# Query and gate strips of 512 columns, and one right operand for the high and low halves

## The chip, the cores and the metric

The kernel runs on one core of a Trainium2 chip. The metric is the device time of one execution in microseconds, the median of several runs. The profile is of one more execution, taken by the hardware profiler. Its engines are TensorE (PE, with its weight loads shown as PEld), VectorE (DVE), ScalarE (ACT), GpSimd (POOL) and SyncE (SP, which here issues the DMAs).

## What is computed

One encoder layer is applied to two sequences: a prompt of 1024 tokens and a sample of 256 tokens, both with the same 16 meta tokens in front. The outputs for the meta tokens are dropped.

```
u = rms_norm(h, norm_w) @ w_in                      # (tokens, 2048) @ (2048, 6656)
qa, ka, va, za, qb, kb, vb, zb = split(u)           # 8, 2, 2, 8, 8, 8, 8, 8 heads of 128
qa, ka = rope(rms_norm(qa)), rope(rms_norm(ka))
ya = softmax(qa ka^T) va * silu(za)                 # global, 4 query heads share a key head
qb, kb = rms_norm(qb), rms_norm(kb)
yb = neighbourhood(qb, kb, vb, bias) * silu(zb)     # window of 8 x 16 tokens, and the meta tokens
y = h + concat(ya, yb) @ w_out
```

Keys and values of the meta tokens are needed. Their queries and gates (z) are not, because their outputs are dropped.

## The kernel before

The input projection is made of 52 strips. A strip is one head's 128 columns of `w_in`, loaded as 16 weight tiles of 128 x 128 (`KT` = 16, the contraction over 2048). The tokens stand in the columns of the right operand. The projection goes over the tokens twice. Chunk one (`chunk1`, line 616) holds 512 columns: the sample's 256 tokens, the prompt's first 240, and the 16 meta tokens at the end. Chunk two (`chunk2`, line 759) holds the prompt's other 784 tokens (`T2`), in a block of 512 and one of 272 (`BL`, line 769), because a PSUM tile of the projection holds 512 columns.

To keep accuracy, each float32 operand is split into a high part in float32r and a low part, the remainder, also in float32r (`split`, line 64). A product is three matmuls into the same PSUM tile: high weights by high x (line 227), high weights by low x (line 228) and low weights by high x (line 229). `strips` (line 192) holds these lines: for each of four weight groups `c` of `WCH` = 4 tiles, for each block `b`, for each of the four tiles `k`, three matmuls.

In chunk one the x tiles are made by `get_x` (line 104) as one tile of `[P, 2, T1]`, high in the first half and low in the second, aligned to 128 bytes. All strips read the first columns of it: k and v strips take all 512 (`B0`, line 636), q and z strips the first 496 (`BQ`). In chunk two `load_all_x` (line 153) makes two tiles for each of the 16 k: `ta` with high and low of the 512 block, and `tb` of 560 columns (`NX`) with the high part of the 272 block in front and the low part in its last 272 columns, from column 288.

A strip's evacuation follows its matmuls. q and k strips go through `qk_evac` (line 257: square, sum over partitions on GpSimd, rotation, reciprocal square root, split), z strips through `z_evac` (line 299: the gate by Exp and Ln), v strips through `v_rows` and transposes. Their results are kept in SBUF or stored to DRAM for later. The PSUM pool `pp` of the projection has four tiles, so a strip of chunk two, which takes two, has its evacuation under the next strip's matmuls.

The order of the work: `chunk1` projects strips and puts the sample's attention of a head between later strips (`later`, `put`, `run_due`). `chunk2` projects, head by head, z and q of the eight global heads, each followed by the head's attention (`attend`, line 366) and one strip of the local heads as filler (`fill`); then come the remaining local strips with the local heads' attention placed between them (`attend_strip`, line 463). The output projection follows (`outproj`, line 1107). The framework's scheduler orders each engine's instructions from this program order, with explicit constraints (`issue_after`, `place_after`). SP issues all the loads and stores in one queue.

The functions that the change touches and what calls them:

Of the kernel before, what the change touches and what calls it, by code (L numbers as in the profile page):

```python
# [21 lines left out]
P = 128  # L22
# [8 lines left out]
T1 = NMETA + NS + C1P  # L31
T2 = NP - C1P
NB = 512
# [26 lines left out]
class Kern:  # L60
# [92 lines left out]
    def load_all_x(self):  # L153
# [3 lines left out]
        for kt in range(KT):  # L157
# [5 lines left out]
            for h, l in ((ta[:, 0], ta[:, 1]), (tb[:, :NT2], tb[:, NX - NT2:])):  # L163
# [9 lines left out]
                o += n  # L173
        self.tc.add_manual_dep(self.qstore, self.xload[KT // 2].name, mybir.DependencyInfo(
# [17 lines left out]
    def strips(self, jobs, getx):  # L192
# [4 lines left out]
        for c in range(KT // WCH):  # L197
# [22 lines left out]
            for b in range(nb)[::-1] if self.turn else range(nb):  # L220
                for k in range(WCH):
                    kt = c * WCH + k
                    xh, xl = getx(kt)[b]
                    first, last = kt == 0, kt == KT - 1
                    for (wh, wl), ps, (_, blocks, _) in zip(ws, out, jobs):
                        p, n = ps[b], blocks[b][1]
                        nc.tensor.matmul(p[:, :n], wh[:, k, :], xh[:, :n], start=first, stop=False)  # L227
                        nc.tensor.matmul(p[:, :n], wh[:, k, :], xl[:, :n], start=False, stop=False)  # L228
                        self.lastmm = nc.tensor.matmul(p[:, :n], wl[:, k, :], xh[:, :n], start=False, stop=last).ins  # L229
# [300 lines left out]
    def rows_out(self, vt, n, dst, o):  # L530

        nc = self.nc
        for a in range(0, n, 4 * P):
# [10 lines left out]
            if f < len(offs):  # L544
# [3 lines left out]
                nc.sync.dma_start(dst[o + n - m:o + n], t[:])  # L548
# [67 lines left out]
    def chunk1(self):  # L616
# [19 lines left out]
        B0, BQ = (0, T1), (0, NS + C1P)  # L636
        PM = NS + C1P

        def kb_strip(s, g, wc):
            kf = self.k.tile([P, T1], F32, tag="k1", name="kcf")  # L640

            def evac(ps):
                self.qk_evac(ps[0], 0, T1, wc, None, [], kf[:])
                nc.sync.dma_start(self.kfd[g][:], kf[:, NS:])
                km = self.k.tile([P, 8, NMETA], F32, tag="km", name="kmf")[:, :3]
                nc.scalar.copy(km, kf[:, PM:].unsqueeze(1).to_broadcast([P, 3, NMETA]))
                return kf, km.rearrange("p c m -> p (c m)")
# [13 lines left out]
        def k_strip(s, g, wc, rope):  # L661
            kt_ = self.k.tile([P, 2, T1], F32R, tag="k1", name="kc1")

            def evac(ps):
                self.qk_evac(ps[0], 0, T1, wc, (ct, st) if rope else None, [(0, T1, kt_[:, 0, :], kt_[:, 1, :])])
                nc.sync.dma_start(self.kd[g][:], kt_[:, :, NS:].bitcast(F32))
                return kt_, self.copy_km(kt_[:, :, PM:])
            return s, [B0], evac

        def v_strip(s, g):  # L670
# [4 lines left out]
            def evac(ps):  # L675
                vt = self.v_rows(ps[0], *B0)
                self.split(vm[:, 0:1, :], vm[:, 1:2, :], self.v_turn(vt, [PM], NMETA))
                if loc:
                    nc.scalar.copy(vs[:], self.v_turn(vt, [0, P]))
                else:  # L680
                    self.split(vs[:, :2, :], vs[:, 2:, :], self.v_turn(vt, [0, P]))
                self.rows_out(vt[:, NS:PM], C1P, self.vn[g], 0)
# [5 lines left out]
        def q_strip(s, h, wc, rope):  # L688
            q = self.s.tile([P, 2, QB], F32R, tag="S", name="qs")

            def evac(ps):
                o, n = BQ
                qp = [self.ev.tile([P, C1P], F32R, tag="ev", name="qp") for _ in range(2)]
                self.qk_evac(ps[0], o, n, wc, (ct[:, o:o + n], st[:, o:o + n]) if rope else None,
                             [(0, NS, q[:, 0, :], q[:, 1, :]), (NS, C1P, qp[0][:], qp[1][:])])
# [5 lines left out]
        def z_strip(s, h):  # L701
            z = self.zlater = self.mx.tile([P, QB], F32, tag="mx", name="zs")

            def evac(ps):
                zp = self.ev.tile([P, C1P], F32, tag="ev", name="zp")
                self.z_evac(ps[0], *BQ, [(0, NS, z[:]), (NS, C1P, zp[:])])
                nc.sync.dma_start(self.zd[h][:, :C1P], zp[:])
# [51 lines left out]
    def chunk2(self):  # L759
# [9 lines left out]
        BL = [(0, NB), (NB, T2 - NB)]  # L769
        self.tie = 0, 0  # L770

# [8 lines left out]
        def k_strip(s, g, wc, rope):  # L780
            k, km = k_first(g)

            def evac(ps):
                for p, (o, n) in zip(ps, BL):
                    rp = (ct[:, o:o + n], st[:, o:o + n]) if rope else None
                    self.qk_evac(p, o, n, wc, rp, [(0, n, k[:, 0, C1P + o:C1P + o + n], k[:, 1, C1P + o:C1P + o + n])])
# [3 lines left out]
        def v_rows_of(s, g):  # L790

            def evac(ps):
                for p, (o, n) in zip(ps, BL):
                    self.rows_out(self.v_rows(p, o, n), n, self.vn[g], C1P + o)
# [21 lines left out]
        def q_strip(s, h, wc, rope):  # L816
            q = self.q.tile([P, 2, NP], F32R, tag="q", name="q", align_bytes=ALIGN)
            nc.sync.dma_start(q[:, :, :C1P].bitcast(F32), self.qd[h][:])

            def evac(ps):  # L820
                for p, (o, n) in zip(ps, BL):
                    rp = (ct[:, o:o + n], st[:, o:o + n]) if rope else None
                    self.qk_evac(p, o, n, wc, rp, [(0, n, q[:, 0, C1P + o:C1P + o + n], q[:, 1, C1P + o:C1P + o + n])])
                return q
            return s, BL, evac

        def z_strip(s, h):
            z = self.z.tile([P, NP], F32, tag="z", name="z")
            nc.sync.dma_start(z[:, :C1P], self.zd[h][:, :C1P])

            def evac(ps):
                for p, (o, n) in zip(ps, BL):
                    self.z_evac(p, o, n, [(0, n, z[:, C1P + o:C1P + o + n])])
                return z
            return s, BL, evac


        def qk_late(s, wc, dst):
            def evac(ps):
                for p, (o, n) in zip(ps, BL):  # L840
                    self.qk_evac(p, o, n, wc, None, [(0, n, dst[:, o:o + n], None)])
            return s, BL, evac

        def z_late(s, dst):
            def evac(ps):
                for p, (o, n) in list(zip(ps, BL))[::-1 if self.turn else 1]:
                    zt = self.ev.tile([P, n], F32, tag="ev", name="zt")
                    self.z_evac(p, o, n, [(0, n, zt[:])])
                    nc.sync.dma_start(dst[:, C1P + o:C1P + o + n], zt[:])
            return s, BL, evac  # L850
# [12 lines left out]
        def q_load(h):  # L863
            qf = self.qf.tile([P, NP], F32, tag="qf", name="qfull")
            nc.sync.dma_start(qf[:, :C1P], self.qfd[h][:])
            nc.sync.dma_start(qf[:, C1P:], self.q2d[h][:])
# [65 lines left out]
        for h in range(NH):  # L932
            v = [v_rows_of(VB + h, 2 + h)]
            kq = [qk_late(KB + h, kwb, self.k2d[2 + h]), qk_late(QB_ + h, qwb, self.q2d[8 + h])]
# [252 lines left out]
    def build(self):  # L1187
# [3 lines left out]
        with tc.tile_pool(name="dr", bufs=1, space=DRAM) as dp, tc.tile_pool(name="const", bufs=1) as cp, \  # L1191
# [5 lines left out]
            self.qd = [dp.tile([P, 2, C1P], F32, name=f"qd{h}") for h in range(8)]  # L1197
            self.qfd = [dp.tile([P, C1P], F32, name=f"qfd{h}") for h in range(16)]
# [145 lines left out]
```

## Time and profile before

| what | value |
|---|---|
| median of 3 runs | 2160.34 us (2159.44 to 2160.65) |
| the profiled execution, its time | 2159.27 us |
| its span in the profile | 2157.5 us |
| granted clock of TensorE | 1.00 |
| PE busy in the span | 2151.3 us |
| DVE, ACT, POOL busy | 1658.5, 1189.0, 522.3 us |

The profile's rows name a line of the kernel, an engine, an operation and its tiles as out<-in, then the shape (partitions x elements), how many there are, the busy time and the mean nanoseconds of one. Matmuls are pipelined: one starts well before the one ahead of it has ended, so the duration of one (390 ns for 512 columns) is no measure of the rate. The distance from one start to the next is. A timeline gives the starts, and its first column is the start in us from the beginning of the span.

### The profile page before, as it was taken

To read this page: it belongs to the slowest core of one execution; us is meant where nothing else is said; L and a number is where in the kernel's file an instruction comes from. 1 tells how busy PE (TensorE), PEld (TensorE's weight loads), DVE (VectorE), ACT (ScalarE), POOL (GpSimd) and SP (SyncE) were. 2 spreads that over 40 slices of the span, in tenths; PEclk is the share of its full clock that TensorE was granted. 3 is DMA by queue.
4 is the path that set the end of the run, shared out by engine and by line. 5 is a ranking of instruction groups with operands and counts; after the bars stand their busy time and mean duration, and the time that the engine had idled before them with its cause. 6 is when DMAs were issued, how large, how long until landed. Compare 5 with 4: busy or idle time off the path is not lost.

```text
span 2157.5 us, 33972 instructions
## 1 busy us (share of the span) xinstructions
PE 2151.3 (100%) x11745; PEld 1877.5 (87%) x11745; DVE 1658.5 (77%) x2989; ACT 1189.0 (55%) x2411; POOL 522.3 (24%) x250
## 2 busy tenths in 40 slices
PE   9999999999999999999999999999999999999999
PEld 7888888888888999999999999998989988888887
DVE  7698976788874899997799998677787886545763
ACT  7677644454565777776677775444443464232230
POOL 1142422222221223231143224324333311000000
PEclk9999999999999999999999999999999999999999
DMA  8666789988664333334332344654443364662663
GB/s 294 216 192 221 241 297 313 331 288 265 214 193 137 94 105 104 106 105 135 98 107 93 104 127 146 188 158 136 130 132 123 115 212 142 239 235 92 234 224 108
DMA packets 257420, 377.24 MB, mean 175 GB/s; under 512 B 43072, under 2 KB 108768, under 8 KB 257248
## 3 DMA queue, kind: packets, MB, share of 16 engines
q1 hardware_dynamic: 257248, 375.07, 53.6%
q8 instruction: 92, 1.51, 0.3%
q14 instruction: 80, 0.66, 0.1%
HBM read 281.01 MB, written 100.38 MB: 177 GB/s over the span
## 4 chain that ended last, share of the span: by engine, by line
PE 99%; DMA 0%; DVE 0%; SPq 0%; issue 0%; ACT 0%
PE pp L227 22%; PE pp L229 22%; PE pp L228 22%; PE pq L1069 6%; PE pq L1068 6%; PE pq L1070 6%; PE po L519 2%; PE sp L485 2%; PE sp L378 1%; PE sp L379 1%; PE sp L377 1%; PE po L420 1%; PE po L419 1%; PE po L418 1%; PE tp L540 0%; PE sp L430 0%
## 5 line engine op out<-in xcount | busy, mean ns | idle before, releaser
L227 PE MATMUL pp<-x,wh 128*128 128x512 f32 (+1 forms) x1664 | 655.0, 395 | 0.9 <-ACT wh L66 0.9
L229 PE MATMUL pp<-x,wl 128*128 128x512 f32 (+1 forms) x1664 | 647.6, 390 | 0.0
L228 PE MATMUL pp<-x,wh 128*128 128x512 f32 (+1 forms) x1664 | 647.1, 389 | 0.0
L229 PEld LDWEIGHTS pp<-x,wl 128*128 128x128 f32 x1664 | 312.4, 188 | 60.9 <-DVE wl L67 0.2
L227 PEld LDWEIGHTS pp<-x,wh 128*128 128x128 f32 x1664 | 312.3, 188 | 59.0 <-ACT wh L66 3.1
L228 PEld LDWEIGHTS pp<-x,wh 128*128 128x128 f32 x1664 | 312.8, 188 | 52.1
L67 DVE TENSOR_TENSOR wl<-wr,wh 128x512 fp32r<-128x512 f32 (+2 forms) x287 | 215.5, 753 | 122.2 <-ACT wh L66 91.3
L262 POOL PARTITION_ALL_REDUCE m<-ms x78 | 222.4, 2852 | 354.3 <-ACT ms L260 293.1
L346 POOL PARTITION_ALL_REDUCE tot<-a x80 | 179.2, 2240 | 435.4 <-DVE a L343 417.1
L66 ACT CAST wh<-wr 128x512 fp32r<-128x512 f32 (+2 forms) x287 | 173.7, 610 | 184.2 <-PE pp L228 170.4
L228 PE MATMUL pp<-xb,wh 128*128 128x272 f32 x832 | 240.7, 289 | 0.0
L227 PE MATMUL pp<-xb,wh 128*128 128x272 f32 x832 | 239.8, 288 | 0.0
L229 PE MATMUL pp<-xb,wl 128*128 128x272 f32 x832 | 239.1, 287 | 0.0
L328 POOL PARTITION_ALL_REDUCE ma<-m x80 | 114.4, 1429 | 448.4 <-DVE m L326 439.7
L1068 PE MATMUL pq<-wm,yh 128*128 128x512 f32 x560 | 218.3, 390 | 0.0
L1070 PE MATMUL pq<-wm,yl 128*128 128x512 f32 x560 | 218.2, 390 | 0.0
L1069 PE MATMUL pq<-wm,yh 128*128 128x512 f32 x560 | 218.0, 389 | 0.0
L227 PEld LDWEIGHTS pp<-xb,wh 128*128 128x128 f32 x832 | 156.5, 188 | 7.5
L228 PEld LDWEIGHTS pp<-xb,wh 128*128 128x128 f32 x832 | 156.5, 188 | 7.5
L229 PEld LDWEIGHTS pp<-xb,wl 128*128 128x128 f32 x832 | 157.4, 189 | 0.3
L1068 PEld LDWEIGHTS pq<-wm,yh 128*128 128x128 f32 x560 | 105.1, 188 | 21.8
L1070 PEld LDWEIGHTS pq<-wm,yl 128*128 128x128 f32 x560 | 105.1, 188 | 21.8
(214 smaller groups left out, 3932.1 us busy)
## 6 DMA issues: line engine op xcount, KB each, us to landing
wr<-in_w_in SPq DMA_DIRECT2D x413, 256.0 KB, 3.4
wld<-wl SPq DMA_DIRECT2D x132, 256.0 KB, 4.2
wl<-wld SPq DMA_DIRECT2D x132, 256.0 KB, 3.1
yr<-yd SPq DMA_DIRECT2D x35, 512.0 KB, 5.1
wq<-in_w_out SPq DMA_DIRECT2D x64, 256.0 KB, 5.0
td<-wq SPq DMA_DIRECT2D x64, 256.0 KB, 4.4
ww<-td SPq DMA_DIRECT2D x64, 256.0 KB, 5.2
ww<-in_w_out SPq DMA_DIRECT2D x48, 256.0 KB, 5.4
```

Of the source, the lines that this page charges most:

```text
L66: self.hi = nc.scalar.copy(hi, full).ins
L67: return nc.vector.tensor_tensor(out=lo, in0=full, in1=hi.bitcast(F32), op=ALU.subtract).ins
L227: nc.tensor.matmul(p[:, :n], wh[:, k, :], xh[:, :n], start=first, stop=False)
L228: nc.tensor.matmul(p[:, :n], wh[:, k, :], xl[:, :n], start=False, stop=False)
L229: self.lastmm = nc.tensor.matmul(p[:, :n], wl[:, k, :], xh[:, :n], start=False, stop=last).ins
L262: nc.gpsimd.partition_all_reduce(m2[:], ms[:], P, RED.add)
L328: nc.gpsimd.partition_all_reduce(ma[:], m1[:], P, RED.max)
L346: nc.gpsimd.partition_all_reduce(tot[:], a1[:], P, RED.add)
L485: nc.tensor.matmul(dst, k[:, o:o + P], qfv[:, a:e, :], start=True, stop=True)
L1068: nc.tensor.matmul(ps, yh, wh, start=k == 0, stop=False)
L1069: nc.tensor.matmul(ps, yh, wl, start=False, stop=False)
L1070: self.lastmm = nc.tensor.matmul(ps, yl, wh, start=False, stop=k == 7).ins
```

## The change

The tokens are put in another order. Chunk one now holds 528 columns: the 16 meta tokens first, then the sample's 256, then the prompt's first 256. k and v strips read the first 512 of them (meta, sample, 240 of the prompt), q and z strips the last 512 (sample, 256 of the prompt). Chunk two holds the prompt's last 768 tokens and after them a second copy of tokens 240 to 255, so again 784 columns. k and v strips take 512 + 272 of them, as before; q and z strips take 512 + 256 (`BQ`).

For a block of 256 columns, line 227 and line 228 become one matmul. Its right operand is a view of `tb` that takes 256 columns from column 0 (high) and 256 from column 288 (low), 512 in all, and it writes the 512 columns of the PSUM tile, so that the high and the low product stand beside each other. The low weights by high x are added to the first 256 columns. Before the evacuation a new helper `whole` copies the second half of the tile to SBUF on ScalarE and adds it to the first half on VectorE.

What is else in the diff follows from the order: stores of k in two pieces (`kd`, `kfd`), k results of the 272 block written in two places (`places`), the buffers for q of 256 columns, and the rope tables and inputs in the new order.

```diff
@@ -28,8 +28,11 @@
 C1P = 240
-T1 = NMETA + NS + C1P
+C1Q = 256
+TK = NMETA + NS + C1P
+T1 = NMETA + NS + C1Q
 T2 = NP - C1P
+N2Q = 256
...
@@ load_all_x
+            b = tb[:]
+            self.xs[kt][1] += (bass.AP(b.tensor, b.offset, [list(b.ap[0]), [NX - NT2, 2], [1, N2Q]]),)
...
@@ strips
-                    xh, xl = getx(kt)[b]
+                    xh, xl, *cat = getx(kt)[b]
                     first, last = kt == 0, kt == KT - 1
                     for (wh, wl), ps, (_, blocks, _) in zip(ws, out, jobs):
-                        p, n = ps[b], blocks[b][1]
-                        nc.tensor.matmul(p[:, :n], wh[:, k, :], xh[:, :n], start=first, stop=False)
-                        nc.tensor.matmul(p[:, :n], wh[:, k, :], xl[:, :n], start=False, stop=False)
+                        p, (o, n) = ps[b], blocks[b]
+                        if not self.second:
+                            xh, xl = (x[:, o:o + n] for x in getx(kt)[b])
+                        if n == N2Q:
+                            nc.tensor.matmul(p[:].rearrange("p (a n) -> p a n", a=2), wh[:, k, :], cat[0], start=first, stop=False)
+                        else:
+                            nc.tensor.matmul(p[:, :n], wh[:, k, :], xh[:, :n], start=first, stop=False)
+                            nc.tensor.matmul(p[:, :n], wh[:, k, :], xl[:, :n], start=False, stop=False)
                         self.lastmm = nc.tensor.matmul(p[:, :n], wl[:, k, :], xh[:, :n], start=False, stop=last).ins
...
@@ chunk1
-        B0, BQ = (0, T1), (0, NS + C1P)
+        B0, BQ = (0, TK), (NMETA, NS + C1Q)
...
             def evac(ps):
-                self.qk_evac(ps[0], 0, T1, wc, None, [], kf[:])
-                nc.sync.dma_start(self.kfd[g][:], kf[:, NS:])
+                self.qk_evac(ps[0], 0, TK, wc, None, [], kf[:])
+                nc.sync.dma_start(self.kfd[g][:, :C1P], kf[:, OP:])
+                nc.sync.dma_start(self.kfd[g][:, C1P:], kf[:, :NMETA])
...
@@ chunk2
-        BL = [(0, NB), (NB, T2 - NB)]
+        BL = [(0, NB), (NB, NT2)]
+        BQ = [(0, NB), (NB, N2Q)]
...
+        def places(n, o):
+            return [(0, min(n, N2Q if o else NB), C1Q + o)] + ([(N2Q, n - N2Q, C1P)] if n == NT2 else [])
+
+        def whole(p, n):
+            if n != N2Q:
+                return p
+            t = self.ev.tile([P, n], F32, tag="ev", name="both")
+            nc.scalar.copy(t[:], p[:, n:])
+            nc.vector.tensor_tensor(out=t[:], in0=p[:, :n], in1=t[:], op=ALU.add)
+            return t
...
+                for p, (o, n) in zip(ps, BQ):
+                    rp = (ct[:, o:o + n], st[:, o:o + n]) if rope else None
+                    d = C1Q + o
+                    self.qk_evac(whole(p, n), o, n, wc, rp, [(0, n, q[:, 0, d:d + n], q[:, 1, d:d + n])])
```

More of the change, by code (lines that the diff above doesn't have):

```diff
@@ L838, in qk_late @@
[L838 to L842, printed above, removed]
+                for p, (o, n) in zip(ps, BQ):
+                    self.qk_evac(whole(p, n), o, n, wc, None, [(0, n, dst[:, o:o + n], None)])
+            return s, BQ, evac
         def z_late(s, dst):
             def evac(ps):
-                for p, (o, n) in list(zip(ps, BL))[::-1 if self.turn else 1]:
+                for p, (o, n) in list(zip(ps, BQ))[::-1 if self.turn else 1]:
```

94 lines of the change are left out of this document (50 added, 44 removed).

## The prediction

> **What bounds the kernel now.** I read the busy times and the chain of waits on the page first, then who made PE wait, then the matmul groups by shape, and last timelines, because they alone give the distance from one matmul's start to the next.
>
> ```profile
> PE 2151.3 (100%) x11745; PEld 1877.5 (87%) x11745; DVE 1658.5 (77%) x2989; ACT 1189.0 (55%) x2411; POOL 522.3 (24%) x250
> ```
>
> ```profile
> PE 99%; DMA 0%; DVE 0%; SPq 0%; issue 0%; ACT 0%
> ```
>
> ```profile
> PE warm L633 <- DVE wz L630: 1.2, 1, 1.2
> PE pp L227 <- ACT wh L66: 0.9, 2, 0.6
> PE tp L296 <- DVE vt L289: 0.3, 1, 0.3
> ```
>
> The chain that ended last is 99% PE, and the matmul stream waited 2.4 us in all for anybody. So the end is set by how long PE takes to feed its matmuls, and a change counts by what it does to their number and width. Three groups matter (each stands three times, for lines 227 to 229):
>
> ```profile
> L228 PE MATMUL pp<-x,wh 128*128 128x512 f32 x1152 | 450.6, 391 | 0.0
> L228 PE MATMUL pp<-xb,wh 128*128 128x272 f32 x832 | 240.7, 289 | 0.0
> ...
> L227 PE MATMUL pp<-x,wh 128*128 128x496 f32 x512 | 197.5, 386 | 0.0
> ```
>
> The 512 of 496 columns are chunk one's 32 q and z strips times 16 k; the 832 of 272 are chunk two's 52 strips, and 32 x 16 = 512 of these belong to q and z. The means (391, 289, 386 ns) are latencies of overlapping instructions: their sum is far over the span, so they price nothing. I take starts instead. Each of the next two fences holds the first and the last start of an unbroken series.
>
> ```profile
> 211.80 0.39 PE L227 MATMUL pp<-x,wh 128*128 128x496 f32 x1
> ...
> 233.02 0.39 PE L229 MATMUL pp<-x,wl 128*128 128x496 f32 x1
> ```
>
> ```profile
> 235.00 0.40 PE L227 MATMUL pp<-x,wh 128*128 128x512 f32 x1
> ...
> 245.69 0.39 PE L229 MATMUL pp<-x,wl 128*128 128x512 f32 x1
> ```
>
> ```profile
> L1068 PE MATMUL pq<-wm,yh x60: 389/389/389, 1999.8 to 2039.9; 128*128 128x512 f32 x60
> ```
>
> A z and a q strip of chunk one are 96 matmuls of 496 columns: 95 distances in 21.22 us, 223.4 ns each. The k strip after them is 48 of 512: 47 in 10.69 us, 227.4 ns. In the output projection, three matmuls for each of the 60 of line 1068 make 177 distances in 40.1 us, 226.6 ns: the steady value for 512. In chunk two twelve of 272 and twelve of 512 alternate:
>
> ```profile
> 641.38 0.29 PE L227 MATMUL pp<-xb,wh 128*128 128x272 f32 x1
> ...
> 642.87 0.39 PE L227 MATMUL pp<-x,wh 128*128 128x512 f32 x1
> ...
> 643.56 0.40 PE L227 MATMUL pp<-x,wh 128*128 128x512 f32 x1
> 643.80 0.39 PE L228 MATMUL pp<-x,wh 128*128 128x512 f32 x1
> ...
> 645.62 0.29 PE L227 MATMUL pp<-xb,wh 128*128 128x272 f32 x1
> ```
>
> The twelve of 272 take 1.49 us, 124.2 ns each; the twelve of 512 take 2.75 us, 229.2 ns, a little over the steady value, and the slowest single one is at 0.24 us. For 256 columns the global attention has a series of 20:
>
> ```profile
> 838.53 0.28 PE L378 MATMUL sp<-q,kf 128*128 128x256 f32 x1
> ...
> 840.92 0.29 PE L227 MATMUL pp<-xb,wh 128*128 128x272 f32 x1
> ```
>
> 2.39 us over 20 is 119.5 ns, every matmul with weights of its own. From 256 to 512 a column costs (226.6 - 119.5) / 256 = 0.418 ns, which leaves 226.6 - 512 x 0.418 = 12.4 ns that a matmul costs whatever its width.
>
> **What the change does to the matmuls.** Per q or z strip and k, before: three of 496 and three of 512 + 272, 3840 columns. After: three of 512, three of 512, one of 512 and one of 256: 3840 columns again. Only the number falls, by 512 over the kernel.
>
> The merge, 512 times: three of 272 become one of 512 and one of 256. By the group's own values 3 x 124.2 = 372.6 ns become 229.2 + 119.5 = 348.7 ns, 23.9 ns saved, 12.2 us. If the twelve of 512 are put at the steady 226.6 and the rest of the period is given to the 272s, these cost more: four periods stand between
>
> ```profile
> 659.14 0.29 PE L227 MATMUL pp<-xb,wh 128*128 128x272 f32 x1
> ...
> 676.12 0.29 PE L227 MATMUL pp<-xb,wh 128*128 128x272 f32 x1
> ```
>
> so one is 4.245 us, less 12 x 0.2266 leaves 1.526 us, 381.5 ns per k; against 226.6 + 119.5 = 346.1 that saves 35.4 ns, 18.1 us. Worst, every merged matmul is as slow as the slowest after a change of width, 240 + 119.5 = 359.5 ns: 13.1 ns, 6.7 us. I take the middle of the two main readings, 15.2 us. That the merged right operand is in two pieces I cost at nothing, by the rows of line 316, where the local heads (`sp`) read q in four pieces of 64 columns and the global heads (`sm_ps`) in one:
>
> ```profile
> L316 PE MATMUL sp<-q,km 128*112 128x256 f32 x32 | 9.0, 282 | 0.0
> L316 PE MATMUL sm_ps<-q,km 128*112 128x256 f32 x32 | 9.0, 282 | 0.0
> ```
>
> The 16 columns more in chunk one, 32 x 16 x 3 = 1536 times: 227.4 - 223.4 = 4.0 ns, 6.1 us lost. From the steady 226.6 it is 3.2 ns, 4.9 us; by the slope 16 x 0.418 = 6.7 ns, 10.3 us. I take 6.1, since both its rows are neighbours in chunk one.
>
> Net: 15.2 - 6.1 = 9.1 us less; bounds 18.1 - 4.9 = 13.2 less and 10.3 - 6.7 = 3.6 more.
>
> The Trainium skill, TensorE: Matmul & The Clock Gate, section Back-to-back issue gap, gives N / 2.4 + 2.5 ns for a warm matmul of N columns. By it the merge saves 3 x 115.8 - (215.8 + 109.2) = 22.5 ns, an estimate of 11.5 us, the 16 columns cost 6.7 ns, 10.2 us, and the kernel would gain 1.3 us. The trace doesn't agree with that fixed part: 226.6 and 119.5 ns stand above 215.8 and 109.2 by about 11 ns each.
>
> **What lies beside PE.** `whole` adds, 32 times, a copy out of PSUM on ACT and an addition on DVE:
>
> ```profile
> L542 ACT COPY vl<-tp 128x256 f32<-128x256 f32 x10 | 3.7, 369 | 6.3 <-PE tp L540 6.3
> ```
>
> ```profile
> L362 DVE TENSOR_TENSOR y<-po,z 128x256 f32<-128x256 f32 x32 | 13.3, 416 | 6.4 <-PE po L421 6.3
> ```
>
> 0.37 + 0.42 = 0.79 us for each, 25 us in all. The addition waits for the copy, and behind it in DVE's queue stand low parts of weights that PE will want. What hides this: a strip of chunk two lasts four periods, 17 us, and PSUM has two strips' tiles. The tightest stage is the global attention:
>
> ```profile
> 698.00:1345.00 647.00, 647.00 (x4194) 592.91 (x4193) 572.91 (x1044) 465.32 (x945) 188.71 (x93) 1.00 0.35 110
> ```
>
> DVE is busy 573 of 647 us there (third sum), ACT 465. Sixteen additions are 6.7 us, so DVE goes from 89% to 90%; the operations behind them shrink from 272 to 256 columns. I cost it at nothing; without that cover it is up to 25 us. SP gets 18 more stores, of 16 columns each, for the 10 k strips of chunk one and the 8 late ones of chunk two. The reload of such a piece occupies the queue for
>
> ```profile
> 613.33 0.56 SPq L777 DMA_DIRECT2D kf<-kd  x1
> ```
>
> so 10 us over the whole kernel, in front of loads of weights for which PE waited nowhere in the list above. The wider x tiles shift memory, so that a load for chunk two may wait for the release of the next k as well, six matmuls or 1.4 us later. The last of these splits starts at 618.6, the first 512 block is read at 630.17, so 11 us cover it:
>
> ```profile
> L167 ACT ACTIVATE x<-x,nw x16: 705/714/726, 597.7 to 618.6; 128x512 fp32r<-128x512 f32 x16
> ```
>
> ```profile
> 630.17 0.40 PE L227 MATMUL pp<-x,wh 128*128 128x512 f32 x1
> ```
>
> **The sum.** The profiled execution took 2159.27 us (span 2157.5); less 9.1 is 2150.2. The median of the runs is 1.1 us above it, so I forecast 2151.3 us, with bounds 2147.1 and 2163.9. About 0.2% (4.3 us) is what a measurement of this kernel can tell from no change.
>
> **Rivals.**
> *Right operands off their alignment (slower).* In chunk one the x tile is aligned to 128 bytes and is now 528 columns or 2112 bytes per half, 16.5 x 128. k and v strips read the low half from 64 bytes past such a boundary, q and z strips the high half, from column 16, twice: 20 x 16 + 32 x 16 x 2 = 1344 matmuls. Before, all reads of x begin on a boundary, so no row shows this. If such a read pays the fixed 12.4 ns once more, that is 16.7 us: 7.6 us slower, 2167.9. It turns the sign from 9.1 / 1344 = 6.8 ns and is slower by over 0.2% from 10 ns. For it: 496 columns are 15.5 x 128 bytes, and 223.4 ns is 3.7 ns above the line 12.4 + 496 x 0.418, so a ragged row may cost; at that price 1344 of them are 5.0 us and the result 2156.3, too near to tell from no change. Against it: 272 columns are 8.5 x 128 bytes and lie on the line (126.1 against 124.2 to 127.2). And line 485 reads a q whose tile the program puts 64 bytes off, line 519 reads an aligned one, at the same length, though in plain float32, at a lower rate:
>
> ```profile
> L519 PE MATMUL po<-S,vw 128*128 128x192 f32 x128 | 26.1, 326 | 0.0
> L485 PE MATMUL sp<-qfull,kfull 128*128 128x192 f32 x128 | 26.0, 326 | 0.0
> ```
>
> The Trainium skill, SBUF — State Buffer, section Specifications (TRN2), puts the engine-side line at 16 bytes; 64 is a whole number of these, so by it the offset costs nothing. No run here shows it.
>
> *Only columns count (no change).* 3840 before and after: if the merged matmul keeps the time of its 816 - 768 = 48 fewer columns alone (20.1 ns, 10.3 us) and the 16 columns cost the slope's 10.3 us, the result is 2160.3. The fixed 12.4 ns speak against it.
>
> *The evacuation comes onto the path (slower).* If DVE's wait for the ACT copy held up a weight split every time, up to 25 us less 9.1: 2176. It decides from 9.1 / 32 = 0.28 us of PE wait for each evacuation; today PE's waits for DVE sum to 1.5 us.
>
> **Chances.** Forecast 0.60, its own range 2147 to 2156. Alignment at the full price 0.15, alignment at the small price 0.13, only columns 0.07, evacuation 0.05. So faster 0.60, same 0.13 + 0.07 = 0.20, slower 0.15 + 0.05 = 0.20. The range for 8 in 10 runs from 2147 to 2166: it takes in the cases without change and part of the alignment's.
>
> **What would show it.** Right: 11233 matmuls in place of 11745; in chunk two's q and z periods a 512 and a 256 about 349 ns apart in sum; chunk one's q and z strips at 227 ns a matmul; waits of PE still near 2.4 us. Wrong: chunk one's series at 235 ns or more (alignment), k strips there too; a 512 of the merged form above 240 ns; PE waiting for `wh`, `wl` or PSUM in the global attention.

## The result and the profile after

The kernel after takes 2182.49 us (median, 2180.57 to 2183.89); the kernel before took 2160.49 us beside it. The ratio is 1.0102, 95% interval 1.009 to 1.0113: 22 us slower, where 9 us less were forecast. The profiled execution took 2182.52 us, span 2180.7.

The page of the kernel after, its busy times and the shares of the chain that ended last:

```profile
PE 2164.6 (99%) x11233; PEld 1843.7 (85%) x11233; DVE 1672.3 (77%) x3023; ACT 1201.2 (55%) x2445; POOL 546.3 (25%) x250
...
PE 87%; DVE 5%; ACT 2%; DMA 2%; POOL 2%; issue 1%; SPq 0%; DVEq 0%; POOLq 0%; ACTq 0%
```

The number of matmuls fell by 512, as it should. By stages: chunk two's first matmul on `xb` starts at 621.8 us (603.7 before), the output projection's first at 1779.5 (1762.4), and the spans end at 2180.7 and 2157.5. So chunk one lost 18.1 us, chunk two won 1.0, and the output projection lost 6.1.

The chain, 99% PE before, now leaves PE for 13% of the span. PE's waits (us in total, times, longest) say where:

```profile
PE pq L1100 <- DVE z L312: 3.2, 1, 3.2
PE pp L237 <- ACT x L170: 2.3, 1, 2.3
PE sp L387 <- DVE mx L397: 2.0, 2, 1.0
PE warm L644 <- DVE wz L641: 1.2, 1, 1.2
PE sm_ps L325 <- DVE mx L397: 1.1, 2, 0.5
```

Only `warm` was there before. New are one wait at the start of the output projection (3.2 us), one at the start of chunk two (2.3 us), and some in the attention of the global heads, near 3 us. (In the kernel after, line 235 is the merged matmul, 237 to 239 are the three plain ones, 1100 to 1102 the output projection, 312 the multiplication in `z_evac`, 170 and 171 the split of x, 169 its load.)

The waits are some 9 of the 22 us. The rest is in the matmul stream itself. The timeline of the kernel after has two unbroken series of 96 matmuls in chunk one. The first is a z and a q strip; the second is a k strip, whose last start is the middle line, and a q strip. First and last start of each:

```profile
217.24 0.39 PE L237 MATMUL pp<-x,wh 128*128 128x512 f32 x1
...
239.10 0.40 PE L239 MATMUL pp<-x,wl 128*128 128x512 f32 x1
...
241.10 0.39 PE L237 MATMUL pp<-x,wh 128*128 128x512 f32 x1
...
251.98 0.39 PE L239 MATMUL pp<-x,wl 128*128 128x512 f32 x1
...
263.02 0.40 PE L239 MATMUL pp<-x,wl 128*128 128x512 f32 x1
```

21.86 us over 95 distances are 230.1 ns for z and q. The k strip takes 10.88 us over 47 distances, 231.5 ns, and the q strip behind it 230.0. Before, 496 columns took 223.4 and the k strip's 512 took 227.4. So q and z pay 6.7 ns a matmul where 4.0 was forecast, and k, on which nothing was changed but the tile it reads, pays 4.1 ns as well.

In chunk two one period (four pairs of the merged form, then twelve matmuls of 512) stands in the timeline like this:

```profile
687.68 0.40 PE L235 MATMUL pp<-xb,wh 128*128 128x512 f32 x1
687.91 0.28 PE L239 MATMUL pp<-xb,wl 128*128 128x256 f32 x1
...
689.09 0.39 PE L237 MATMUL pp<-x,wh 128*128 128x512 f32 x1
...
691.86 0.40 PE L235 MATMUL pp<-xb,wh 128*128 128x512 f32 x1
```

Four pairs take 1.41 us, 352.5 ns each (forecast 348.7). The twelve of 512 take 2.77 us, 230.8 ns each (229.2 before). The period is 4.18 us (the median of some 32 periods that stand unbroken too) against 4.245 before: 0.065 us less. If all 32 strips x 4 periods were like it, that would be 8.3 us, where 15.2 us were forecast.

### The profile page after: what moved, and what is told of

Its sections match the earlier page's. It is cut to its first block, busy times and chain, and to the rows that moved or that the text cites. A ratio compares the mean times of both kernels' runs of the same rounds, so it can differ in the third digit from the quotient of the medians.

```text
span 2180.7 us, 33024 instructions
## 1 busy us (share of the span) xinstructions
PE 2164.6 (99%) x11233; PEld 1843.7 (85%) x11233; DVE 1672.3 (77%) x3023; ACT 1201.2 (55%) x2445; POOL 546.3 (25%) x250
## 4 chain that ended last, share of the span: by engine, by line
PE 87%; DVE 5%; ACT 2%; DMA 2%; POOL 2%; issue 1%; SPq 0%; DVEq 0%; POOLq 0%; ACTq 0%
PE pp L239 19%; PE pp L237 17%; PE pp L238 17%; PE pq L1100 6%; PE pq L1101 6%; PE pq L1102 6%; PE pp L235 4%; PE po L529 2%; PE sp L495 2%; PE sp L387 1%; PE po L430 1%; PE sp L388 1%; PE sp L389 1%; PE po L429 1%; PE po L428 1%
## 5 line engine op out<-in xcount | busy, mean ns | idle before, releaser
L237 PE MATMUL pp<-x,wh 128*128 128x512 f32 x1664 | 661.6, 399 | 3.1 <-ACT x L170 2.3
L239 PE MATMUL pp<-x,wl 128*128 128x512 f32 x1664 | 655.9, 395 | 0.0
L238 PE MATMUL pp<-x,wh 128*128 128x512 f32 x1664 | 651.5, 392 | 0.0
L272 POOL PARTITION_ALL_REDUCE m<-ms x78 | 241.8, 3100 | 340.4 <-ACT ms L270 271.1
L70 DVE TENSOR_TENSOR wl<-wr,wh 128x512 fp32r<-128x512 f32 (+2 forms) x287 | 203.7, 711 | 133.0 <-ACT wh L69 98.4
L356 POOL PARTITION_ALL_REDUCE tot<-a x80 | 189.8, 2373 | 449.0 <-DVE a L353 424.8
L239 PE MATMUL pp<-xb,wl 128*128 128x256 f32 (+1 forms) x832 | 235.0, 283 | 0.0
L235 PE MATMUL pp<-xb,wh 128*128 128x512 f32 x512 | 188.8, 397 | 0.0
L1100 PEld LDWEIGHTS pq<-wm,yh 128*128 128x128 f32 x560 | 105.5, 188 | 26.1 <-issue 3.5
L1101 PEld LDWEIGHTS pq<-wm,yh 128*128 128x128 f32 x560 | 105.6, 188 | 21.7
L235 PEld LDWEIGHTS pp<-xb,wh 128*128 128x128 f32 x512 | 96.1, 188 | 19.4
L408 ACT ACTIVATE S<-S 128x512 f32<-128x512 f32 x136 | 84.5, 630 | 38.6 <-DVE S L407 38.6
```

The source lines that it names most:

```text
L70: return nc.vector.tensor_tensor(out=lo, in0=full, in1=hi.bitcast(F32), op=ALU.subtract).ins
L235: nc.tensor.matmul(p[:].rearrange("p (a n) -> p a n", a=2), wh[:, k, :], cat[0], start=first, stop=False)
L272: nc.gpsimd.partition_all_reduce(m2[:], ms[:], P, RED.add)
L356: nc.gpsimd.partition_all_reduce(tot[:], a1[:], P, RED.add)
L1100: nc.tensor.matmul(ps, yh, wh, start=k == 0, stop=False)
L1101: nc.tensor.matmul(ps, yh, wl, start=False, stop=False)
```

## The experiments

Each ran beside the kernel before; ratios are to it. The theory grew with the runs and ended with four parts: the 16 columns; the place of the x tiles in memory, once for the address at which an operand begins (**place**) and once for which tile of chunk two lies on which of chunk one (**overlap**); the helper `whole`; and the merged matmul, which isn't cheaper than what it replaces. The rivals were the prediction's alignment rival (64 bytes past a multiple of 128), the width of the tile by itself, and the fixed cost of 12.4 ns for every matmul.

### The wider x tile alone, without and with an offset of 64 bytes

```diff
-            t = self.x.tile([P, 2, T1], ...)
-            h, l = t[:, 0, :], t[:, 1, :]
+            t = self.x.tile([P, 2, T1 + 32], ...)
+            h, l = t[:, 0, 0:0 + T1], t[:, 1, 0:0 + T1]      # e1; 16:16 + T1 in e2
```

> The kernel before, with chunk one's x tile made 32 columns wider per half (544) and read from its first column as before: every right operand stays on a 128-byte boundary and no matmul changes. Theory M (memory): chunk two's first x tile now lies over chunk one's last one (k = 15), so its load waits for chunk one's last matmuls; PE then waits 2 to 4 us for the split at the boundary and runs some us at a lower clock: 2163 to 2167 us. Theory R (ragged right operands) alone: 2160 to 2161 us, distances of 227 ns for 512 columns as before.

> As e1, but the data begins at column 16 of each half, so that all 2496 matmuls of chunk one read from 64 bytes past a 128-byte boundary. Theory R: each costs 3 to 5 ns more (the change showed about 3.5 ns on its high by high matmuls), 7 to 12 us above e1, with distances of 230 to 232 ns for 512 columns and 225 to 227 for 496. The rival of the prediction at its full price, 12.4 ns: 31 us above e1. If alignment is free: the time of e1.

Measured: 2172.20 us (1.0052, 1.0035 to 1.0068) and 2172.93 us (1.0056, 1.0041 to 1.0071). A tile that is wider and otherwise unused costs 11.5 us, half of the loss, and more than either theory had for the first run; the 64 bytes beyond it cost nothing that can be measured. The alignment rival falls in the form in which it was stated: the first run loses though all its reads begin at a multiple of 128 bytes. (That the second run's reads are free isn't shown, since the first isn't free either; see the place of the x tile.) The first one's series of a z and a q strip and of the k strip after them, as in the kernel before, and its longest wait of PE:

```profile
213.60 0.39 PE L227 MATMUL pp<-x,wh 128*128 128x496 f32 x1
...
234.92 0.39 PE L229 MATMUL pp<-x,wl 128*128 128x496 f32 x1
...
236.91 0.39 PE L227 MATMUL pp<-x,wh 128*128 128x512 f32 x1
...
247.77 0.39 PE L229 MATMUL pp<-x,wl 128*128 128x512 f32 x1
```

```profile
PE pp L227 <- ACT x L167: 2.4, 1, 2.4
```

21.32 / 95 = 224.4 and 10.86 / 47 = 231.1 ns, against 223.4 and 227.4: a longer distance though the reads begin at multiples of 128 bytes. And the wait at the start of chunk two is there. So the tile does two different things.

### 512 columns for q and z, nothing else

```diff
-            return s, [BQ], evac
+            return s, [B0], evac          # in the three q and z strips of chunk one
```

> The kernel before, with chunk one's q and z matmuls over all 512 columns in place of 496 (the meta tokens' too, which are not used); evacuation of 496 as before. It prices the 16 columns alone, aligned. By the trimmed distances of before (222.1 for 496, 227.4 for 512) 5.3 ns x 1536 = 8.1 us: 2168 us. By the prediction's row 4.0 ns, 6.1 us: 2166.5 us. If what chunk one lost in the change is alignment and memory alone: 2160 to 2163 us.

Measured: 2169.18 us (1.0038, 1.0023 to 1.0053), 8.4 us more, 5.5 ns for each of the 1536 matmuls. The mechanism of this term was right, its size in the prediction was 6.1. Its series of a z and a q strip, first and last start:

```profile
214.48 0.40 PE L227 MATMUL pp<-x,wh 128*128 128x512 f32 x1
...
236.04 0.39 PE L229 MATMUL pp<-x,wl 128*128 128x512 f32 x1
```

21.56 us over 95 distances are 226.9 ns. The prediction's row for 496 columns, 223.4 ns, is one pair of strips; a q strip that follows a k strip in the kernel before (starts from 245.91 to 256.25) takes 220.0 ns.

### `whole` left out

```diff
             if n != N2Q:
                 return p
-            t = self.ev.tile([P, n], F32, tag="ev", name="both")
-            nc.scalar.copy(t[:], p[:, n:])
-            nc.vector.tensor_tensor(out=t[:], in0=p[:, :n], in1=t[:], op=ALU.add)
-            return t
+            return p
```

> The changed kernel, with whole left out: the second half of the PSUM tile (high weights by low x of the 256 block of q and z) is not added. PE's work is the same. Theory E (evacuation): the wait of 3.2 us at the start of the output projection, the low clock after it and the waits of about 3 us in the global attention go, 6 to 10 us: 2173 to 2177 us. Theories R and M: these waits come from elsewhere, 2181 to 2183 us.

Measured: 2172.98 us (1.0056, 1.0041 to 1.0071), 9.5 us less than the kernel after. The two operations of 0.79 us, 32 times, weren't hidden. The longest waits of PE in this run:

```profile
PE pp L237 <- ACT x L170: 2.3, 1, 2.3
PE sm_ps L325 <- DVE mx L397: 1.5, 2, 0.7
```

The wait at the output projection is gone, the one at the chunk boundary isn't; of the waits for `mx` and `Sm`, results of DVE in the global attention, 2.7 us remain without `whole`. From its first matmul to the end of the span the output projection takes 395.0 us, as before (395.1), and 401.2 in the kernel after, where the granted clock is also 0.71 from 1790 to 1795 us, as the wait ends; this is 6.2 of the 9.5 us. What `whole` did there is seen in the timeline of the kernel after, where the last z strip gives up its PSUM:

```profile
1776.16 0.28 PE L239 MATMUL pp<-xb,wl 128*128 128x256 f32 x1
...
1782.49 0.36 ACT L793 COPY both<-pp 128x256 f32<-128x256 f32 x1
...
1784.15 0.42 DVE L794 TENSOR_TENSOR both<-pp,both 128x256 f32<-128x256 f32 x1
...
1786.29 0.42 DVE L312 TENSOR_TENSOR z<-both,rb 128x256 f32<-128x256 f32 x1
...
1789.96 0.68 DVE L312 TENSOR_TENSOR z<-pp,rb 128x512 f32<-128x512 f32 x1
...
1790.78 0.47 PE L1100 MATMUL pq<-wm,yh 128*128 128x512 f32 x1 [3.20 <-DVE z L312]
```

The small block is done on PE at 1776.4. Its copy, its addition and its multiplication each stand in a queue behind other work, 6, 1.3 and 1.7 us, and the large block's multiplication, which lets PSUM go, comes last. In the kernel before the small block needs no copy:

```profile
1759.54 0.28 PE L229 MATMUL pp<-xb,wl 128*128 128x272 f32 x1
...
1760.27 0.44 DVE L302 TENSOR_TENSOR z<-pp,rb 128x272 f32<-128x272 f32 x1
```

Its multiplication starts 0.7 us after the block's last matmul. So it isn't the 0.79 us of the two operations that count but two more turns in queues. DVE stood for the copy in 8 of the 32 times, 9.8 us in all:

```profile
DVE both L794 <- ACT both L793: 9.8, 8, 4.2
```

### The place of the x tile

The addresses here and below are those that the program gives its tiles, in bytes within a partition. In the kernel before, the program puts chunk one's x tiles 4096 bytes apart from address 157440 on, and both halves begin at a multiple of 256. In the first experiment the low half begins 128 past one. In the kernel after the tiles are 4224 bytes apart, so that every other one begins 128 past a multiple of 256, the low half 64 further, q's and z's reads 64 further again.

```diff
-            t = self.x.tile([P, 2, T1], ...)
-            h, l = t[:, 0, :], t[:, 1, :]
+            t = self.x.tile([P, 2, 576], ...)
+            h, l = t[:, 0, 0:0 + T1], t[:, 1, 0:0 + T1]      # e5; 32:32 + T1 in e6
```

> The kernel before, with chunk one's x tiles 576 columns wide instead of 528 (data from column 0), so that the high half starts at a multiple of 256 bytes and the low half too (2304 bytes further), as they do in the kernel before (2112 bytes wide rows in tiles padded to 4096). Theory 'place': what made the first experiment's chunk one slower (224.5 to 225.1 ns for 496 columns and 231.1 to 232.5 for 512, against 222 and 227.4 to 228.4 before) is where in a row of 256 bytes an operand begins; with both halves at 0 the distances are back at 222 and 227 to 228, and only the cost at the chunk boundary is left (the first x load of chunk two waits for chunk one's last matmul): 2164 to 2166 us. Rival 'width': any tile that is wider than before has the higher distances, 225 and 231 to 232: 2172 us.

> The kernel before, chunk one's x tiles 576 columns wide and the data from column 32, so that both halves start 128 bytes past a multiple of 256. Theory 'place', in the form that the place itself counts: all distances are as in the first experiment, 225 and 231 to 232, 2172 us. In the form that only a difference between the places of the high and the low half counts: 222 and 227 to 228, 2164 to 2166 us. Rival 'width': 2172 us, and the same as the run without the offset.

(A row of the kernel before is 2048 bytes wide, not 2112; its halves begin at a multiple of 256 all the same.) Measured: 2165.57 us (1.0023, 1.0014 to 1.0033) and 2175.23 us (1.0067, 1.0052 to 1.0082). The same two series, first of the fifth run, then of the sixth:

```profile
211.56 0.39 PE L227 MATMUL pp<-x,wh 128*128 128x496 f32 x1
...
232.78 0.39 PE L229 MATMUL pp<-x,wl 128*128 128x496 f32 x1
...
234.77 0.40 PE L227 MATMUL pp<-x,wh 128*128 128x512 f32 x1
...
245.45 0.39 PE L229 MATMUL pp<-x,wl 128*128 128x512 f32 x1
```

```profile
214.40 0.38 PE L227 MATMUL pp<-x,wh 128*128 128x496 f32 x1
...
235.91 0.39 PE L229 MATMUL pp<-x,wl 128*128 128x496 f32 x1
...
237.90 0.39 PE L227 MATMUL pp<-x,wh 128*128 128x512 f32 x1
...
248.82 0.39 PE L229 MATMUL pp<-x,wl 128*128 128x512 f32 x1
```

223.4 and 227.2 ns where both halves begin at a multiple of 256, the values of the kernel before in a tile that is wider still; 226.4 and 232.3 ns where both begin 128 bytes past one. Same shapes, same tile, same order of work, 9.7 us apart. The width rival falls, and so does the form in which only a difference between the halves counts: the address itself counts. The Trainium skill, SBUF — State Buffer, section Specifications (TRN2), gives lines of 16 bytes on the engine side; by that rule alone both places would cost the same, and these runs disagree. Why 256 is the boundary stays open.

In the fifth run chunk one runs as before, so its 5.0 us lie elsewhere: overlap, below.

```diff
             t = self.x.tile([P, 2, 576], ...)
-            h, l = t[:, 0, :], t[:, 1, :]                    # of the kernel after
+            h, l = t[:, 0, 48:48 + T1], t[:, 1, 48:48 + T1]
```

> The kernel after, chunk one's x tiles 576 columns wide and the data from column 48 instead of 544 and 16, so that the 512 columns that q and z read start at a multiple of 256 bytes in both halves, and k's and v's 64 bytes before one. Theory 'place': q's and z's 1536 matmuls fall from 229 to 232 ns to 227.4 to 228.4, chunk one's projection from 580 to some 575 us, and the time to some 2177 us. Rival 'width': nothing changes, 2182 us.

(What is moved is a tile of 528 columns, of which q and z read from column 16.) Measured: 2180.04 us (1.0091, 1.0074 to 1.0108), 2.5 us less than after, half of what was expected. The series of z and q, and of k (to the middle line) and q:

```profile
215.95 0.40 PE L237 MATMUL pp<-x,wh 128*128 128x512 f32 x1
...
237.51 0.40 PE L239 MATMUL pp<-x,wl 128*128 128x512 f32 x1
...
239.51 0.39 PE L237 MATMUL pp<-x,wh 128*128 128x512 f32 x1
...
250.47 0.39 PE L239 MATMUL pp<-x,wl 128*128 128x512 f32 x1
...
261.40 0.40 PE L239 MATMUL pp<-x,wl 128*128 128x512 f32 x1
```

z and q, now at a multiple of 256, are back at 226.9 ns, those of the third experiment, and the q strip of the second series is at 227.7. But k, 64 bytes before such a multiple in both halves, went up from 231.5 to 233.2. The means over all of chunk one, from the starts in the timelines (distances between neighbours of the stream, without those over 290 ns, which are waits or a record that is missing), with the bytes past a multiple of 256 at which the high and the low half are read:

| run | q and z: columns | high, low | ns | k and v: high, low | ns |
|---|---|---|---|---|---|
| before | 496 | 0, 0 | 222.1 | 0, 0 | 227.9 |
| fifth | 496 | 0, 0 | 222.2 | 0, 0 | 227.9 |
| first | 496 | 0, 128 | 224.8 | 0, 128 | 231.7 |
| second | 496 | 64, 192 | 225.7 | 64, 192 | 230.4 |
| sixth | 496 | 128, 128 | 226.1 | 128, 128 | 232.4 |
| third | 512 | 0, 0 | 227.0 | 0, 0 | 228.1 |
| after | 512 | 64, 128 or 192, 0 | 230.3 | 0, 64 or 128, 192 | 231.5 |
| seventh | 512 | 0, 0 | 227.5 | 192, 192 | 233.3 |

The seventh run wins 2.8 ns on 1536 matmuls, 4.3 us, and loses 1.8 ns on 960, 1.7 us: 2.6 us, the measured 2.5. Each run with a half that begins elsewhere than at a multiple of 256 pays 2.5 to 5.2 ns a matmul. The second run pays too, and so it is as slow as the first. In the kernel after the place costs 3.3 x 1536 + 3.4 x 960 ns = 8.3 us against the third run's means.

### Which tile lies on which

In the kernel before, chunk two's x tile 0 takes the address of chunk one's tile 0, and so on to 15. With wider tiles in chunk one the addresses shift. The pool gives its lowest place to the tile that is written first and fills the others from the top down. So tile 0 of chunk two (157440 to 161536 in the kernel after) lies on the end of chunk one's tile 0 and the start of its tile 15 (159616 to 163840): the first to be loaded waits for the last to be read. The loads of x in SP's queue in the kernel before (duration min/median/max, first and last start):

```profile
L166 SPq DMA_DIRECT2D xb<-x2d x16: 422/430/467, 581.5 to 591.0; - x16
...
L166 SPq DMA_DIRECT2D x<-x2d x16: 360/382/1316, 592.3 to 610.3; - x16
```

and in the kernel after, with the wait of the queue:

```profile
L169 SPq DMA_DIRECT2D x<-x2d x16: 319/424/706, 617.5 to 642.3; - x16
L169 SPq DMA_DIRECT2D xb<-x2d x16: 320/426/1569, 617.9 to 643.3; - x16
```

```profile
SPq L169 <- PE pp L239: 15.4, 1, 15.4
```

The queue stands 15.4 us at the first load, for chunk one's last matmul, with the other 31 loads behind it; the last of them starts 33 us later than before, while chunk one itself ends 18 us later. PE then waits for the first split.

```diff
+        tas = {kt: self.x.tile([P, 2, NB], ...) for kt in (KT - 1, *range(KT - 1))}
         for kt in range(KT):
...
-            ta = self.x.tile([P, 2, NB], ...)
+            ta = tas[kt]
```

> The kernel after, with one edit: chunk two's 16 x tiles are allocated with tile 15 first, so that its first-loaded tile no longer lies on the memory of chunk one's last-read tile. Theory: TensorE's wait of 2.3 us at the chunk boundary and the half clock behind it go, and SP's wait of 15.4 us for chunk one's last matmul; 3 to 5 us less, 2177 to 2179 us. Rival: the wait has another cause and stays: 2182 us.

Measured: 2182.38 us (1.01, 1.0085 to 1.0115), the time of the kernel after. The edit didn't do what it says: a place is given at a tile's first write, not where it is declared, and tile 0 had the address 157440 again. So it is a second run of the kernel after, and SP's wait of 15.4 us stands in it too. It tells one other thing. The granted clock (the last but two of the columns) in the stretch after the boundary wait, in the kernel after and then in this run:

```profile
620.00:625.00 5.00, 3.96 (x12) 3.17 (x13) 3.09 (x6) 3.82 (x8) 0.00 (x0) 0.66 0.93 286
```

```profile
620.00:626.00 6.00, 3.60 (x16) 2.57 (x16) 2.77 (x6) 3.50 (x7) 0.00 (x0) 1.00 0.91 278
```

After the same wait of 2.3 us the clock was once half for a part of 5 us and once not, at the same total time. At the first matmul after the wait this run is 1.3 us behind the kernel after; by 625 us, after the half clock of the other, 0.3 us; by 643 us, after small waits and one of 0.8 us for a load (`po <- DMA vm<-vmd`), 1.4 us again. So what the half clock takes there, about 1 us, the run without it loses again while the last x tiles are still being loaded.

For the next run a write of one element is what comes first:

```diff
+        tl = self.x.tile([P, 2, NB], ...)
+        nc.gpsimd.memset(tl[:1, 0, :1].bitcast(F32), 0.0)
         for kt in range(KT):
...
-            ta = self.x.tile([P, 2, NB], ...)
+            ta = tl if kt == KT - 1 else self.x.tile([P, 2, NB], ...)
```

> The kernel before with chunk one's x tiles 576 wide (the fifth run) and one more edit: a one-element write of GpSimd to chunk two's last x tile comes first in the program, so that this tile takes the lowest place of the pool, the one over chunk one's last-read tile, and tile 0 the highest. Theory 'overlap': all that the fifth run was slower by comes from tile 0 waiting for chunk one's last matmul; its loads now start while chunk one still runs, TensorE's wait of 2.3 us at the chunk boundary is gone, and the time is that of the kernel before, 2160.5 to 2162 us. Rival (the wider tile costs something by itself): 2165.5 us and the wait stays, or the wait goes and 3 us remain.

Measured: 2162.95 us (1.0012, 1.0002 to 1.0021), 2.6 us less than the fifth run. The tile is at the lowest address, PE's wait at the boundary is gone (0.3 us is left), the loads start at 587.0. The overlap is shown for half of the 5.0 us; SP still waits 13.4 us for PE, now behind its third load, because xb tile 1 of chunk two (155008 to 157248) lies on chunk one's wider tile 15 (153856 to 158464). Of the rival (the wider tile costs something by itself, 3 us remain) the number nearly came, 2.4 us, but not the cause: chunk two starts at 603.6 as before, so chunk one loses nothing, and the run falls back 2.0 us from there to 628, where the x tiles are still being loaded. That fits the second overlap; no run takes it away.

### The merge undone

```diff
-                        if n == N2Q:
+                        if n == 0:
...
-            if n != N2Q:
-                return p
...
+            return p
```

> The kernel after with the merge alone undone: the 256 columns of chunk two's q and z go by three matmuls of 256 columns, and `whole` has no copy and add. Theory 'columns': a matmul of 256 columns takes 117 ns, three take 352, and the merged pair takes 235 + 117 = 352, so the merge brought nothing and cost what `whole` costs, 9.5 us by the fourth run: 2173 us, no wait of TensorE at the output projection. Rival (the recorded prediction's fixed cost of 12.4 ns a matmul): three matmuls are 10 ns longer than the pair, 5 us over 512 triples, 2178 us.

Measured: 2168.56 us (1.0039, 1.0024 to 1.0053), 13.9 us less than the kernel after, and more than the 9.5 us of `whole`. One period of it:

```profile
687.90 0.28 PE L237 MATMUL pp<-xb,wh 128*128 128x256 f32 x1
...
689.31 0.39 PE L237 MATMUL pp<-x,wh 128*128 128x512 f32 x1
...
692.03 0.28 PE L237 MATMUL pp<-xb,wh 128*128 128x256 f32 x1
```

Twelve of 256 columns take 1.41 us, 117.5 ns each, as long as the four merged pairs. And the twelve of 512 behind them take 2.72 us, 226.7 ns each, where they take 230.8 beside the merged form. The period is 4.13 us, as in the median of the 33 that stand unbroken. If all 128 were like it, the gain would be 0.115 x 128 = 14.7 us, near the forecast 15.2, of which the merge would give 0.05 x 128 = 6.4 us back. Over chunk two as a whole, from its first matmul on `xb` to the first of the output projection, this run takes 1148.6 us and the fifth, which has the same late loads at the start, 1160.9: 12.3 us less. And by the times of the runs the merge without `whole` costs 13.9 - 9.5 = 4.4 us. Either way the gain of chunk two comes from 272 columns becoming 256, for the number of matmuls here is that of the kernel before. The rival with the fixed cost falls.

### Of the change only the new order

> The kernel after with the merge undone (tenth run), x tiles 576 wide and read from column 48 (seventh run), and the last x tile at the pool's base (ninth run): of the change only the new order of the tokens is left, and k's and v's operands at 192 bytes past a multiple of 256. By the terms so far: 2160.5 + 8.4 (16 more columns in chunk one) - 1536 x 7.8 ns = 12.0 (272 to 256 columns in chunk two) + 960 x 3.5 ns = 3.4 (k's and v's place) = 2160.3 us. Rival: the attention's part pays for the new order as well (it took 704.6 us against 693.1 in the profiles of after and before, of which the named waits are some 7): 2164 us or more.

Its edits are those of the tenth, seventh and ninth runs together. Measured: 2163.99 us (1.0018, 1.0009 to 1.0028), still slower than before, 3.7 us above what was expected. From the tenth run's 2168.56 the seventh run's 2.5 and the ninth's 2.6 lead to 2163.5, so the edits add up. The expectation was low because it took the overlap for fully cured and k's and v's place for 3.5 ns where it is 5.2 (233.3 against 228.1). The total is the one that the rival named, but the attention isn't what pays: in chunk two its matmuls take 265.8 us from start to next start, waits included, and 265.6 in the kernel before.

### The merged operand from another tile

```diff
-            self.xs[kt][1] += (bass.AP(b.tensor, b.offset, [list(b.ap[0]), [NX - NT2, 2], [1, N2Q]]),)
+            self.xs[kt][1] += (ta[:, :, :N2Q],)
```

> The kernel after, the merged operand taken from the 512-column x tile (the first 256 columns of its high and of its low half, both at a multiple of 256 bytes) instead of the tile of the 256 block, whose high half starts 128 bytes past one; the output of that block is thus that of other tokens' high half. Theory 'place': the merged matmul falls from 235 ns to 230 or less, 2.6 us or more in all: 2179 to 2180 us. Rival 'pieces': the 235 ns come from the operand being in two pieces, and stay: 2182.5 us.

Measured: 2182.22 us (1.0102, 1.0086 to 1.0117), no change that can be measured. The stream moved all the same. One period:

```profile
689.11 0.39 PE L234 MATMUL pp<-x,wh 128*128 128x512 f32 x1
...
690.51 0.39 PE L236 MATMUL pp<-x,wh 128*128 128x512 f32 x1
...
693.25 0.39 PE L234 MATMUL pp<-x,wh 128*128 128x512 f32 x1
```

4.14 us in place of 4.18: with both pieces at a multiple of 256 the pair is at 350 ns and the 512s at 228.3, nearly what the undone form has. So place has a part in the merged form's price, but the total doesn't bear it out: 0.04 x 128 = 5 us would be expected, and chunk two as a whole takes 1156.4 us in place of 1157.7. The wait at the output projection is 3.7 us in place of 3.2.

This run stays inconclusive.

## Why the prediction was wrong

By terms, in us, each from a run: 16 more columns +8.4 (third); chunk two's 256 in place of 272 columns -12.3 (tenth against fifth, chunk two as a whole); the merge +4.4 (tenth against fourth); `whole` +9.5 (fourth); overlap and what goes with it at the chunk boundary +5.0 (fifth); the place of chunk one's operands +8.3 (the means of the table). Together 23.3 where 22.0 were measured. The forecast was 9.1 less. `whole` (+9.5), the place (+8.3) and the overlap (+5.0) stood in its sum at nothing; the merge with its columns brought 7.9 in place of 15.2, and the 16 columns cost 2.3 more than they were given. All five went the same way.

- **"I take the middle of the two main readings, 15.2 us"** (the merge) failed in its reason; the 12.3 - 4.4 = 7.9 us that came lie inside the bounds given, 6.7 to 18.1, which is luck. It was priced as 512 matmuls fewer, at a fixed 12.4 ns each. The triple of 256 takes 3 x 117.5 = 352.5 ns and the pair takes 352.5: two matmuls made one brought nothing. The whole gain came from the columns, 1.49 us for twelve of 272 against 1.41 for twelve of 256. The 12.4 ns were a line through two rows from different stages; 117.5 and 226.7 ns, as they stand in the tenth run's chunk two, give 8.3, and the merged form didn't even save that. The rival "Only columns count" had this term's cause right. No group of 256 in chunk two was in the trace of before. The Trainium skill's N / 2.4 + 2.5 ns (TensorE: Matmul & The Clock Gate, Back-to-back issue gap), which it gives for an isolated matmul, made the saving an estimate of 11.5 us, 20.0 of its 22.5 ns from the columns; its reason was the better one, though its figures stay below the 226.7 and 117.5 ns measured here.
- **"I take 6.1, since both its rows are neighbours in chunk one"** (the 16 columns): right mechanism, wrong size, 8.4. The row of 223.4 ns was not the usual one: the mean over chunk one's 496 columns is 222.1. The bounds, 4.9 to 10.3, held it.
- **"`whole` ... I cost it at nothing"** failed. The cover named was the next strip of 17 us; but behind the last z strip stands the output projection, which wants its PSUM at once, and the price is that of two more turns in full queues, not of 0.79 us. At the output projection that is shown (6.2 us); for the other 3.3 us, in chunk two, the same cause is likely and not shown. The condition that the rival stated (0.28 us for each evacuation) is just about what was measured, 9.5 / 32 = 0.30 us; it had a chance of 0.05.
- **"a load for chunk two may wait for the release of the next k as well"**, with 11 us of cover, failed. It isn't the next k but the last, for the first tile, and the queue keeps order behind it: 15.4 us. Working out the addresses would have shown it.
- **"If such a read pays the fixed 12.4 ns once more"** (the alignment rival, at nothing in the sum) had the kind of cause right and its rule wrong. The boundary is 256 bytes and not 128, so that reads which it took for aligned pay as well (first run: 128 past, 2.7 and 3.8 ns), and the price is 3 to 5 ns and not 12.4. Its small price, 3.7 ns, was nearly the mean measured, 3.3 and 3.4, but was laid on 1344 matmuls and not on all 2496 of chunk one. It also hit k's and v's reads, as its own mark said ("k strips there too"), at 231 ns and not at 235.
- **The signs to watch** did their work: PE's waits rose from 2.4 us, for PSUM and for DVE, as the text said a wrong prediction would show.

## What to carry to other kernels

Merging two matmuls that share weights saved nothing here at 256 columns each, where the time went with the columns; measure the narrow one in its own stage before paying an extra copy and addition for it. A change of a tile's size is a change of addresses: work out where each operand then begins, and which tile of the next stage lies on which of this one, above all for the first load in a queue. Evacuation that is hidden inside a loop is bare at the loop's last turn, where the next stage wants the same PSUM.

## What the hardware showed unasked

A float32r right operand of 512 columns is read at 227.2 ns a matmul from addresses at a multiple of 256 bytes and at 232.3 ns from 128 past one; 496 columns at 223.4 and 226.4 (fifth and sixth run). Nothing else differs between the two kernels.

The half clock came and stayed away after equal waits of PE (2.3 us; 0.66 and 1.00 in the rows above). At half clock the matmuls of 512 columns stand 0.43 us apart, from 621.04 to 624.62. The Trainium skill (TensorE: Matmul & The Clock Gate, What's actually happening) has the activity counted in free-running windows of about 3.4 us. That fits the length, and that equal waits differ. Its table there has the clock fall after at least one idle window; here it fell after a wait of 2.3 us, shorter than one.
